# Last projection, norm and stores in two halves of 256 columns, with the second chunk's norm and the last gate on the vector engine

## The chip, the cores and the metric

The kernel runs on one core of a Trainium2 chip. The core has five engines that work side by side, each through its own list of instructions in the order in which the program gives them: TensorE (PE, matrix products), VectorE (DVE), ScalarE (ACT), GpSimd (POOL) and SyncE (SP, which here only issues transfers). Semaphores tie the lists together. Transfers between the core's memory and the chip's main memory go through 16 DMA engines; ACT can issue some too. The metric is the device time of one execution in microseconds (us).

## The reference

A trunk of two layers over 2048 positions of 1024 numbers each. The first layer is a gated short convolution. The second is a stick-breaking attention of 8 heads of 64, strictly causal, whose result is gated, projected back to 1024, added to the residual stream and normed:

```python
def _rmsnorm(x, g):
    xf = x.astype(jnp.float32)
    y = xf * lax.rsqrt(jnp.mean(xf * xf, axis=-1, keepdims=True) + RMS_EPS)
    return (y * g.astype(jnp.float32)).astype(x.dtype)
...
        z = jnp.einsum("bhqd,bhkd->bhqk", qb, kf[:, :, :kl]) * scale
        q_pos = q0 + jnp.arange(Q_BLOCK)
        mask = jnp.arange(kl)[None, :] < q_pos[:, None]
        log_one_minus = jnp.where(mask, jax.nn.log_sigmoid(-z), 0.0)
        rev = lax.cumsum(log_one_minus, axis=3, reverse=True)
        weights = jnp.exp(jnp.where(mask, z + rev, -jnp.inf))
        outs.append(jnp.einsum("bhqk,bhkd->bhqd", weights, vf[:, :, :kl]))
```

All numbers are float32. The change is in the very last steps: gate, output projection, residual addition, final norm, stores.

## The kernel before

**Layout.** Features lie on the 128 partitions, positions along the columns. The positions are cut into four chunks of 512, c = 0 to 3, which are worked in this order; the last chunk, c = 3, is the one with which the program ends. The residual stream of a chunk is 8 tiles of 128 x 512 (`x2_c_i` holds two of them; `x` in the profile). A float32 product is made of three products of parts: each operand is split into a high and a low part (`mm3`: high by high, high by low, low by high), so an output tile of the last projection is 4 x 3 = 12 matmuls of 512 columns, and a chunk has 8 x 12 = 96.

**Attention.** For each chunk and head, `attend` makes the scores (`z`), the scan (`R`), its transposes (`wt`, split into `wth` and `wtl`) and the products with the values (`av`). The result of a pair of heads is a tile `ot`; `gate_kept` adds a first-value term (`v_first`) and multiplies by the gate (`sga`), and for c of 2 and 3 splits it into `og` (high and low part), the operand of the projection. The program's order is not the order of the heads: head 7's second half of chunk 3 is the last to be done.

**Projection and norm.** `out_kept` (c = 0 to 2) makes the 8 product tiles (`pob`), adds each to its `x` on DVE, squares it on ACT (`sq`), sums the squares on POOL (`acc`) and scales by the gain on ACT. `norm_kept` sums `acc` over the partitions with PE (`pst`: products with a column of ones), takes the reciprocal root by 12 small DVE steps (`v`, `t`, `yr`), spreads it over the partitions by four transposes (`prb`), multiplies the 8 tiles and stores them by SP. The multiplication is POOL's for c of 0 and 1, from a copy of `prb` (`pbs`) that ACT makes, and DVE's for c = 2, straight from `prb`.

`out_last` does both for c = 3: squares of the first five tiles are summed by POOL into `acc`, those of the other three go to PE straight away, so that PE does four tiles of sums at the end. Its multiplications are six by DVE and two (k = 2 and 6) by POOL, which reads a second broadcast copied by ACT. Its stores go in turn to SP and ACT.

**What sets the order.** Every operation is first recorded with the name of its part: `a37` is head 7 of chunk 3, `g33` the gate of its fourth tile, `o2` and `n2` projection and norm of chunk 2, `o3` the last projection with its norm. `places` gives each operation a number, between the two numbers of its part in the table PLAN; `order` then runs through all operations with estimated durations, always takes the one that can start first (by that number where several can), and so fixes one list for each engine. `emit` (line 363) writes them out, so line 363 stands in every row of the profile. Behind all of them the program reads a flag (`some`) and branches on it (line 1409); the branch isn't taken in this run.

Of the kernel before, what the change touches and what calls it, by code (L numbers as in the profile page):

```python
# [10 lines left out]
F32 = mybir.dt.float32  # L11
# [5 lines left out]
P = 128  # L17
# [354 lines left out]
def kernel(  # L372
# [891 lines left out]
    def gate_kept(c, k, ot):  # L1264
        sg = load_sg(c, k)
        by_block = ot.rearrange("p (j k) -> p j k", j=4)
        nc.gpsimd.tensor_add(by_block, by_block, v_first[:, c, k, :].unsqueeze(2).to_broadcast([P, 4, P]))
        nc.gpsimd.tensor_mul(ot, ot, sg)
        if c < 2:
            nc.sync.dma_start(out=og_d[c][k], in_=ot)  # L1270
        else:
            split_og(c, k, ot)
# [31 lines left out]
    def norm_kept(c):  # L1304
        pb = rstd_bcast(acc_b[c], f"x2{c}")
        if c < 2:
            pbs = t512(f"pbs_{c}")
            nc.scalar.copy(pbs, pb)
        for k, x in enumerate(x2_t[c]):
            if c < 2:  # L1310
                nc.gpsimd.tensor_mul(x, x, pbs)
            else:
                nc.vector.tensor_mul(x, x, pb)
            nc.sync.dma_start(out=outT[k * P:(k + 1) * P, cols(c)], in_=x)

    def out_last(c):

        x2 = x2_rows(c)
        acc = sb.tile([P, CH], F32, name=f"acc_x2{c}", tag="acc", bufs=2)
        ps2 = psum.tile([P, CH], F32, name=f"pst_x2{c}", tag="wt", bufs=NWT)  # L1320

        def add_sums(t, first, last):
            for j in range(4):
                nc.tensor.matmul(ps2[:, j:j + 1], t[:, j * P:(j + 1) * P], ones[:, 0:1], start=first and j == 0,
                                 stop=last and j == 3, skip_group_check=True)

        late = []
        for ob in range(KD):
            x = x2[ob]
            nc.sync.dma_start(out=x, in_=x1_d[c][ob])  # L1330
            tag, bufs = (("lin", NLIN), ("z", NZ))[ob % 2]
            ps = psum.tile([P, CH], F32, name=f"pob_{c}_{ob}", tag=tag, bufs=bufs)
            mm3(ps, wob[ob:ob + 1], og_t[c], kt=4)
# [5 lines left out]
            if ob < NACC:  # L1339
                square_into(acc, x, ob == 0, f"x2{c}{ob}", nc.gpsimd, ("wth", NWTS))  # L1340
            else:
                sq = sb.tile([P, CH], F32, name=f"sq_x2{c}{ob}", tag=("wth", "wtl")[ob % 2], bufs=NWTS)
                nc.scalar.activation(sq, x, AF.Square)
                late.insert(0, sq)
# [3 lines left out]
        y = rsqrt(ps2, f"x2{c}")  # L1348
        pb = bcast(y, f"x2{c}")
        pbs = t512(f"pbs_{c}")  # L1350
        nc.scalar.copy(pbs, bcast(y, f"x2{c}s"))
        for k in range(KD):
            if k in (2, 6):
                nc.gpsimd.tensor_mul(x2[k], x2[k], pbs)
            else:
                nc.vector.tensor_mul(x2[k], x2[k], pb)
            (nc.scalar if k % 2 else nc.sync).dma_start(out=outT[k * P:(k + 1) * P, cols(c)], in_=x2[k])
# [45 lines left out]
    part("o3", out_last, 3)  # L1403
# [43 lines left out]
```

## Time and profile before

| what | before |
|---|---|
| median of 3 runs | 1345.77 us (1344.04, 1347.22, 1345.77) |
| the profiled execution's own time | 1344.17 us |
| its span (first to last record) | 1342.4 us |
| PE busy | 1304.5 us, 97% |
| weight loads (PEld, beside PE) | 1079.2 us, 80% |
| DVE busy | 1015.8 us, 76% |
| ACT busy | 599.3 us, 45% |
| POOL busy | 435.6 us, 32% |
| DMA | 364.99 MB, mean 272 GB/s |

The share of busy time is over the whole span; the change touches its last 100 us. In the rows below and in the prediction, a group reads `out<-in` with the program's names, then partitions x elements; `x8` is a count; a releaser behind `<-` is what ended the idle time ahead of an instruction. A window's row gives its length, then busy time and count of PE, PEld, DVE, ACT and POOL, the granted PE clock as a share of full speed, the busy share of the DMA engines and the GB/s moved.

### The profile page before, as it was taken

To read this page: it belongs to the slowest core of one execution; us is meant where nothing else is said; L and a number is where in the kernel's file an instruction comes from. 1 tells how busy PE (TensorE), PEld (TensorE's weight loads), DVE (VectorE), ACT (ScalarE), POOL (GpSimd) and SP (SyncE) were. 2 spreads that over 40 slices of the span, in tenths; PEclk is the share of its full clock that TensorE was granted. 3 is DMA by queue.
4 is the path that set the end of the run, shared out by engine and by line. 5 is a ranking of instruction groups with operands and counts; after the bars stand their busy time and mean duration, and the time that the engine had idled before them with its cause. 6 is when DMAs were issued, how large, how long until landed. Compare 5 with 4: busy or idle time off the path is not lost.

```text
span 1342.4 us, 18964 instructions
## 1 busy us (share of the span) xinstructions
PE 1304.5 (97%) x6182; PEld 1079.2 (80%) x6182; DVE 1015.8 (76%) x1605; ACT 599.3 (45%) x1052; POOL 435.6 (32%) x553
## 2 busy tenths in 40 slices
PE   7999999999999999999999999999999999999996
PEld 5788888888888888888787778788778887788885
DVE  6899866689964654656869569877998886797855
ACT  7344434444431332223344334554555553566643
POOL 5252000001000000010032355234456675547982
PEclk9999999999999999999999999999999999999997
DMA  9539879878898799987999976887687567998734
GB/s 288 207 106 326 285 278 318 295 263 312 287 358 291 253 348 340 336 272 246 351 328 310 307 260 214 259 275 237 220 297 261 186 203 225 339 363 304 266 103 161
DMA packets 216348, 364.99 MB, mean 272 GB/s; under 512 B 18096, under 2 KB 102064, under 8 KB 216240
## 3 DMA queue, kind: packets, MB, share of 16 engines
q1 hardware_dynamic: 214464, 362.61, 79.5%
q10 hardware_dynamic: 1616, 1.05, 0.3%
q8 instruction: 51, 0.84, 0.2%
q14 instruction: 57, 0.47, 0.1%
q0 software_dynamic: 160, 0.02, 0.1%
HBM read 217.35 MB, written 146.28 MB: 271 GB/s over the span
## 4 chain that ended last, share of the span: by engine, by line
PE 79%; DVE 11%; issue 3%; DMA 3%; POOL 1%; ACT 1%; SPq 0%; DVEq 0%; POOLq 0%; ACTq 0%
PE fa_C L363 11%; PE fa_B L363 10%; PE pob L363 6%; PE fa_o L363 6%; PE fd_C L363 6%; PE fa_kq L363 5%; PE fd_B L363 5%; PE fa_vg L363 4%; PE fe_C L363 3%; PE fd_o L363 3%; PE fd_vg L363 3%; PE fe_B L363 3%; PE fd_kq L363 3%; PE av L363 2%; PE wt L363 2%
## 5 line engine op out<-in xcount | busy, mean ns | idle before, releaser
L363 POOL COPY halo<-p 128x2 f32<-128x2 f32 x32 | 15.1, 472 | 435.9 <-DVE p L363 435.8
L363 POOL TENSOR_TENSOR acc_x<-acc_x,sq_x 128x512 f32<-128x512 f32 x53 | 76.0, 1438 | 129.6 <-ACT sq_x L363 124.9
L363 PE MATMUL pob<-og,wob 128*128 128x512 f32 x384 | 103.9, 404 | 0.6 <-DVE x L363 0.6
L363 PE MATMUL fa_C<-op_t,whl_s_C 128*128 128x512 f32 x336 | 83.3, 390 | 0.0
L363 PE MATMUL fa_B<-op_t,whl_s_B 128*128 128x512 f32 x336 | 82.4, 390 | 0.2 <-ACT f_B L363 0.2
L363 PEld LDWEIGHTS pob<-og,wob 128*128 128x128 f32 x384 | 67.6, 189 | 11.9 <-DVE x L363 1.1
L363 DVE TENSOR_TENSOR_SCAN R<-R,ones 128x192 f32<-128x192 f32 x128 | 74.2, 621 | 3.2 <-POOL R L363 3.2
L363 PEld LDWEIGHTS fa_B<-op_t,whl_s_B 128*128 128x128 f32 x336 | 62.9, 188 | 13.6 <-ACT f_B L363 0.6
L363 PEld LDWEIGHTS fa_C<-op_t,whl_s_C 128*128 128x128 f32 x336 | 63.0, 188 | 13.1
L363 DVE SCALAR_TENSOR_TENSOR cv<-p,cw,cv 128x512 f32<-128x512 f32 x64 | 50.4, 788 | 11.0 <-ACT cv L363 8.4
L363 ACT CAST wth<-wt 128x512 fp32r<-128x512 f32 x64 | 36.5, 573 | 39.1 <-PE av L363 21.6
L363 ACT ACTIVATE sq_x<-x 128x512 f32<-128x512 f32 x56 | 35.1, 631 | 42.1 <-DVE x L363 30.9
L363 ACT ACTIVATE cv<-p,cw 128x512 f32<-128x512 f32 x32 | 23.2, 725 | 68.1 <-DVE p L363 68.1
L363 DVE TENSOR_TENSOR wtl<-wt,wth 128x512 fp32r<-128x512 f32 x64 | 42.5, 668 | 13.1 <-ACT wth L363 12.2
L363 PE MATMUL wt<-ident,R 128*128 128x128 f32 x248 | 46.6, 275 | 1.4 <-DVE R L363 1.4
L363 PE MATMUL fa_C<-op_b,whl_a_C 128*128 128x512 f32 x168 | 43.1, 390 | 0.0
L363 PE MATMUL fa_B<-op_t,whl_a_B 128*128 128x512 f32 x168 | 43.0, 390 | 0.0
L363 PE MATMUL fe_B<-op_b,whl_a_B 128*128 128x512 f32 x168 | 42.9, 390 | 0.0
L363 POOL TENSOR_SCALAR_AFFINE_SELECT R<-R 128x256 f32<-128x256 f32 x64 | 34.5, 547 | 24.7 <-ACT R L363 24.4
L363 PE MATMUL fd_C<-op_t,whl_s_C 128*128 128x512 f32 x168 | 42.3, 390 | 0.1
L363 PE MATMUL fe_C<-op_b,whl_a_C 128*128 128x512 f32 x168 | 42.0, 390 | 0.0
L363 PE MATMUL fd_C<-op_b,whl_s_C 128*128 128x512 f32 x168 | 41.8, 390 | 0.0
(1016 smaller groups left out, 3813.4 us busy)
## 6 DMA issues: line engine op xcount, KB each, us to landing
sw_s_C<-whl_s_C SPq DMA_DIRECT2D x32, 512.0 KB, 4.2
sw_s_B<-whl_s_B SPq DMA_DIRECT2D x32, 512.0 KB, 4.4
q<-q_d SPq DMA_DIRECT2D x32, 512.0 KB, 5.9
sw_a_C<-whl_a_C SPq DMA_DIRECT2D x24, 512.0 KB, 3.5
sw_a_B<-whl_a_B SPq DMA_DIRECT2D x24, 512.0 KB, 3.7
whl_s_C<-sw_s_C SPq DMA_DIRECT2D x24, 512.0 KB, 5.4
whl_s_B<-sw_s_B SPq DMA_DIRECT2D x24, 512.0 KB, 5.3
whl_s_o<-sw_s_o SPq DMA_DIRECT2D x24, 512.0 KB, 5.3
```

The source lines that it names most:

```text
L363: getattr(o.engine.engine, o.name)(*map(real, o.args), **{k: real(v) for k, v in o.kw.items()})
```

## The change

The last projection (`out_last`) is done twice, for columns 0 to 255 and for 256 to 511 of the last chunk, each time with its own sums, root, broadcast, multiplications and stores. A product tile is now 128 x 256, so there are 192 matmuls of 256 columns in place of 96 of 512, with a weight load each as before. A half has two columns of sums instead of four (`add_sums`), a root of two columns, a broadcast of two transposes. All eight multiplications of a half are DVE's; the second broadcast with its copy (`pbs`) and POOL's two multiplications are gone. The first half stores by SP alone, the second in turn by SP and ACT; a store is 128 KB, with rows of 1 KB.

The second chunk's norm (c = 1) is multiplied by DVE instead of POOL. The last gate (c = 3, k = 3) is done by DVE in four steps of 128 columns that add and multiply at once, instead of POOL's addition and multiplication. In PLAN, `o3` becomes `o30` and `o31`, and the numbers of `a06`, `a30`, `a31`, `a36`, `o0` and `o1` change.

```diff
@@ -54,19 +54,19 @@
...
-    "n2": (1218.33, 1322.06), "o3": (2272.7, 2273.2),
+    "n2": (1218.33, 1322.06), "o30": (2272.7, 2272.95), "o31": (2272.95, 2278.2),
...
@@ -1263,9 +1263,15 @@
 
     def gate_kept(c, k, ot):
         sg = load_sg(c, k)
-        by_block = ot.rearrange("p (j k) -> p j k", j=4)
-        nc.gpsimd.tensor_add(by_block, by_block, v_first[:, c, k, :].unsqueeze(2).to_broadcast([P, 4, P]))
-        nc.gpsimd.tensor_mul(ot, ot, sg)
+        if c == NCH - 1 and k == 3:
+            for b in range(4):
+                blk = slice(b * P, (b + 1) * P)
+                nc.vector.scalar_tensor_tensor(out=ot[:, blk], in0=ot[:, blk], scalar=v_first[:, c, k, b:b + 1],
+                                               in1=sg[:, blk], op0=ALU.add, op1=ALU.mult)
+        else:
+            by_block = ot.rearrange("p (j k) -> p j k", j=4)
+            nc.gpsimd.tensor_add(by_block, by_block, v_first[:, c, k, :].unsqueeze(2).to_broadcast([P, 4, P]))
+            nc.gpsimd.tensor_mul(ot, ot, sg)
         if c < 2:
             nc.sync.dma_start(out=og_d[c][k], in_=ot)
         else:
@@ -1303,58 +1309,64 @@
 
     def norm_kept(c):
         pb = rstd_bcast(acc_b[c], f"x2{c}")
-        if c < 2:
+        if c < 1:
             pbs = t512(f"pbs_{c}")
             nc.scalar.copy(pbs, pb)
         for k, x in enumerate(x2_t[c]):
-            if c < 2:
+            if c < 1:
                 nc.gpsimd.tensor_mul(x, x, pbs)
             else:
                 nc.vector.tensor_mul(x, x, pb)
             nc.sync.dma_start(out=outT[k * P:(k + 1) * P, cols(c)], in_=x)
 
-    def out_last(c):
-
-        x2 = x2_rows(c)
-        acc = sb.tile([P, CH], F32, name=f"acc_x2{c}", tag="acc", bufs=2)
-        ps2 = psum.tile([P, CH], F32, name=f"pst_x2{c}", tag="wt", bufs=NWT)
+    HC = CH // 2
+    x2_last = []
+
+    def out_last(c, hf):
+
+        if hf == 0:
+            x2_last.extend(x2_rows(c))
+            for ob in range(KD):
+                nc.sync.dma_start(out=x2_last[ob], in_=x1_d[c][ob])
+        at = slice(hf * HC, (hf + 1) * HC)
+        nm = f"x2{c}{hf}"
+        acc = sb.tile([P, CH], F32, name=f"acc_{nm}", tag="acc", bufs=2)[:, 0:HC]
+        ps2 = psum.tile([P, CH], F32, name=f"pst_{nm}", tag="wt", bufs=NWT)
 
         def add_sums(t, first, last):
-            for j in range(4):
+            for j in range(2):
                 nc.tensor.matmul(ps2[:, j:j + 1], t[:, j * P:(j + 1) * P], ones[:, 0:1], start=first and j == 0,
-                                 stop=last and j == 3, skip_group_check=True)
+                                 stop=last and j == 1, skip_group_check=True)
 
         late = []
         for ob in range(KD):
-            x = x2[ob]
-            nc.sync.dma_start(out=x, in_=x1_d[c][ob])
+            x = x2_last[ob][:, at]
             tag, bufs = (("lin", NLIN), ("z", NZ))[ob % 2]
-            ps = psum.tile([P, CH], F32, name=f"pob_{c}_{ob}", tag=tag, bufs=bufs)
-            mm3(ps, wob[ob:ob + 1], og_t[c], kt=4)
+            ps = psum.tile([P, CH], F32, name=f"pob_{c}_{ob}_{hf}", tag=tag, bufs=bufs)[:, 0:HC]
+            mm3(ps, wob[ob:ob + 1], [og[:, :, at] for og in og_t[c]], kt=4)
             if late:
                 add_sums(late.pop(), ob == NACC + 1, False)
             if ob == NACC:
                 late.append(acc)
             nc.vector.tensor_add(x, x, ps)
-            if ob < NACC:
-                square_into(acc, x, ob == 0, f"x2{c}{ob}", nc.gpsimd, ("wth", NWTS))
+            if ob == 0:
+                nc.scalar.activation(acc, x, AF.Square)
             else:
-                sq = sb.tile([P, CH], F32, name=f"sq_x2{c}{ob}", tag=("wth", "wtl")[ob % 2], bufs=NWTS)
+                sq = sb.tile([P, CH], F32, name=f"sq_{nm}{ob}", tag=("wth", "wtl")[ob % 2], bufs=NWTS)[:, 0:HC]
                 nc.scalar.activation(sq, x, AF.Square)
-                late.insert(0, sq)
+                if ob < NACC:
+                    nc.gpsimd.tensor_add(acc, acc, sq)
+                else:
+                    late.insert(0, sq)
             nc.scalar.activation(x, x, AF.Copy, scale=gains["f"][:, ob:ob + 1])
         while late:
             add_sums(late.pop(), False, not late)
-        y = rsqrt(ps2, f"x2{c}")
-        pb = bcast(y, f"x2{c}")
-        pbs = t512(f"pbs_{c}")
-        nc.scalar.copy(pbs, bcast(y, f"x2{c}s"))
+        pb = bcast(rsqrt(ps2, nm, n=2), nm, n=2)[:, 0:HC]
+        o = S - CH * (c + 1) + hf * HC
         for k in range(KD):
-            if k in (2, 6):
-                nc.gpsimd.tensor_mul(x2[k], x2[k], pbs)
-            else:
-                nc.vector.tensor_mul(x2[k], x2[k], pb)
-            (nc.scalar if k % 2 else nc.sync).dma_start(out=outT[k * P:(k + 1) * P, cols(c)], in_=x2[k])
+            x = x2_last[k][:, at]
+            nc.vector.tensor_mul(x, x, pb)
+            (nc.scalar if hf and k % 2 else nc.sync).dma_start(out=outT[k * P:(k + 1) * P, o:o + HC], in_=x)
 
 
     def part(name, f, *args):
@@ -1400,7 +1412,8 @@
     for c in range(3):
         part(f"o{c}", out_kept, c)
         part(f"n{c}", norm_kept, c)
-    part("o3", out_last, 3)
+    for hf in range(2):
+        part(f"o3{hf}", out_last, 3, hf)
     nc.on = False
     ops = nc.order(PLAN)
     with tc.manual_schedule():
```

Three places show what this does to the lists of instructions. In the names, the number behind a tile is a counter; `pob_7` before is the eighth product tile, `pob_7_1` after the eighth of the second half.

PE, end of the program. Before, the last product tile is followed by four tiles of sums with four columns each, and by two broadcasts:

```order
L363 MATMUL pob_7_13128<-og_3_13025,wob_11711 128x512 x3
L363 MATMUL pst_x_13150<-ones,acc_x_13058 128x1 x4
L363 MATMUL pst_x_13150<-ones,sq_x_13139 128x1 x4
L363 MATMUL pst_x_13150<-ones,sq_x_13152 128x1 x4
L363 MATMUL pst_x_13150<-ones,sq_x_13163 128x1 x4
L363 MATMUL prb_x_13189<-ident,yr_x_13178 128x128 x4
L363 MATMUL prb_x23s<-ident,yr_x_13178 128x128 x4
```

After, the end of the second half:

```order
L363 MATMUL pst_x_13312<-ones,acc_x_13197 128x1 x2
L363 MATMUL pob_7_1_13317<-og_0_12837,wob_11711 128x256 x3
L363 MATMUL pob_7_1_13317<-og_1_12568,wob_11711 128x256 x3
L363 MATMUL pob_7_1_13317<-og_2_12712,wob_11711 128x256 x3
L363 MATMUL pob_7_1_13317<-og_3_13021,wob_11711 128x256 x3
L363 MATMUL pst_x_13312<-ones,sq_x_13322 128x1 x2
L363 MATMUL pst_x_13312<-ones,sq_x_13328 128x1 x2
L363 MATMUL pst_x_13312<-ones,sq_x_13344 128x1 x2
L363 MATMUL prb_x_13364<-ident,yr_x_13353 128x128 x2
```

The first of four tiles of sums now stands ahead of the last product tile, each tile has two columns, and there is one broadcast of two transposes. All sums and the broadcast of the first half stand further up, among the second half's products.

DVE, from the split of the last attention's weights to the last gate (`ot_3`). Before:

```order
L363 TENSOR_TENSOR wtl_6_1_12901<-wt_6_1_12882,wth_6_1_12893 128x512
L363 TENSOR_TENSOR x_2_3_12629<-x_2_3_12629,pob_7_12880 128x512
L363 TENSOR_TENSOR wtl_7_1_12934<-wt_7_1_12889,wth_7_1_12927 128x512
L363 TENSOR_TENSOR ot_3_12931<-ot_3_12931,av_6_12783 64x512
L363 TENSOR_TENSOR ot_3_12931<-ot_3_12931,av_7_12949 64x512
L363 TENSOR_SCALAR v_x_13023<-pst_x_13016 128x4
```

After:

```order
L363 TENSOR_TENSOR wtl_6_1_12861<-wt_6_1_12841,wth_6_1_12850 128x512
L363 TENSOR_TENSOR x_1_0_12012<-x_1_0_12012,prb_x_12857 128x512 x2
L363 TENSOR_TENSOR x_1_1_12073<-x_1_1_12073,prb_x_12857 128x512 x2
L363 TENSOR_TENSOR x_1_2_12160<-x_1_2_12160,prb_x_12857 128x512 x2
L363 TENSOR_TENSOR x_1_3_12194<-x_1_3_12194,prb_x_12857 128x512 x2
L363 TENSOR_TENSOR x_2_2_12563<-x_2_2_12563,pob_5_12830 128x512
L363 TENSOR_TENSOR x_2_3_12591<-x_2_3_12591,pob_6_12872 128x512
L363 TENSOR_TENSOR wtl_7_1_12933<-wt_7_1_12883,wth_7_1_12911 128x512
L363 TENSOR_TENSOR ot_3_12919<-ot_3_12919,av_6_12805 64x512
L363 TENSOR_TENSOR x_2_3_12591<-x_2_3_12591,pob_7_12930 128x512
L363 TENSOR_TENSOR ot_3_12919<-ot_3_12919,av_7_12950 64x512
L363 SCALAR_TENSOR_TENSOR ot_3_12919<-ot_3_12919,v_first,sga_3_11075 128x128 x4
```

The eight multiplications of the second chunk's norm (`x_1_0` to `x_1_3`) now stand ahead of the split `wtl_7_1` of the last head, and the gate stands behind the two additions to `ot_3` as four steps.

PE, around the first use of `og_3`, the last gate's result. Before, from the third chunk's sums on:

```order
L363 MATMUL pst_x_13016<-ones,acc_x_12704 128x1 x4
L363 MATMUL pob_5_13006<-og_1_12608,wob_11669 128x512
L363 MATMUL pob_5_13006<-og_2_12710,wob_11669 128x512 x3
L363 MATMUL pob_0_12924<-og_3_13025,wob_11312 128x512
L363 MATMUL pob_1_12947<-og_3_13025,wob_11330 128x512
L363 MATMUL pob_2_12979<-og_3_13025,wob_11367 128x512
L363 MATMUL pob_3_12994<-og_3_13025,wob_11628 128x512
L363 MATMUL pob_0_12924<-og_3_13025,wob_11312 128x512 x2
L363 MATMUL pob_1_12947<-og_3_13025,wob_11330 128x512 x2
```

After:

```order
L363 MATMUL pst_x_13011<-ones,acc_x_12673 128x1 x4
L363 MATMUL pob_5_0_13018<-og_0_12837,wob_11669 128x256 x3
L363 MATMUL pob_5_0_13018<-og_1_12568,wob_11669 128x256 x3
L363 MATMUL pob_5_0_13018<-og_2_12712,wob_11669 128x256 x2
L363 MATMUL pob_0_0_12970<-og_3_13021,wob_11312 128x256
L363 MATMUL pob_1_0_12907<-og_3_13021,wob_11330 128x256
L363 MATMUL pob_2_0_12987<-og_3_13021,wob_11367 128x256
L363 MATMUL pob_3_0_12925<-og_3_13021,wob_11628 128x256
L363 MATMUL pob_5_0_13018<-og_2_12712,wob_11669 128x256
L363 MATMUL pob_5_0_13018<-og_3_13021,wob_11669 128x256
L363 MATMUL pob_0_0_12970<-og_3_13021,wob_11312 128x256 x2
L363 MATMUL pob_1_0_12907<-og_3_13021,wob_11330 128x256 x2
```

In both, the products with `og_3` are put off behind those of other tiles that need only `og_0` to `og_2`; after, those tiles are half as wide, so the same count of products lasts half as long.

10 rows, old and new, of the table PLAN are left out of this document.

## The prediction

> **What bounds the kernel now.** I read the stretches of the span first, then the chain of work that ended last, then the queues of the last 40 us. The stretches (length, then busy time and count of PE, PEld, DVE, ACT and POOL, granted clock, DMA share, GB/s) say where TensorE (PE) stops being full:
>
> ```profile
> 1315.00:1324.00 9.00, 9.00 (x46) 7.54 (x44) 7.57 (x13) 6.49 (x12) 5.17 (x4) 1.00 0.65 234
> 1324.00:1343.00 19.00, 5.08 (x34) 4.62 (x33) 5.75 (x19) 2.39 (x4) 2.49 (x2) 0.56 0.33 116
> ```
>
> Up to 1324 PE is busy all the time; behind it lie 19 us in which it does 5. So there are two regions: a dense stream, which gets shorter only by less matrix work, and a tail of dependent steps. The chain (start, length, what) shows their border:
>
> ```profile
> core 0 of [0], span 1342.4 us
> ...
> 1301.31 1.11 PE av L363 x10
> 1302.42 7.11 PE pob L363 x31
> 1309.53 0.79 PE pst_x L363 x8
> 1310.31 4.42 PE pob L363 x19
> 1314.73 0.44 PE prb_x L363 x4
> 1315.17 8.22 PE pob L363 x36
> 1323.39 3.76 PE pst_x L363 x32
> 1327.15 0.02 issue
> 1327.18 0.17 DVE v_x L363
> ...
> 1329.66 1.10 PE prb_x L363 x4
> ...
> 1330.85 0.70 DVE x L363
> ```
>
> From 1301.31 to 1323.39 each PE piece begins where the one before it ends: no wait is left in the stream. Call 1323.39, the end of the last projection matmul, **E**. Behind E: sums of squares on PE (3.76 us), the reciprocal root on DVE (1327.18 to 1329.66), its broadcast by PE (to 1330.85), the multiplications, the last store. The last multiplication is POOL's, and the last store of the SP queue waits for it:
>
> ```profile
> 1334.82 0.33 SPq L363 DMA_DIRECT2D out_dram<-x  x1
> ```
> The span ends at 1342.4, 7.58 us after that issue. Three rows say what lies in between: the landing of the last SP store (KB, us from issue), the queue's wait behind it, and the DMA engines (share, GB/s) in those microseconds:
>
> ```profile
> out_dram<-x SPq DMA_DIRECT2D x1, 256.0 KB, 5.2
> ```
> ```profile
> SPq L1409 <- SPq L1409: 3.8, 1, 3.8
> ```
> ```profile
> 1334.00:1338.00 4.00, 0.00 (x0) 0.00 (x0) 0.53 (x1) 0.00 (x0) 0.79 (x1) 0.50 1.02 370
> ```
>
> Line 1409 is the program's closing read of a flag and its branch, which SP does once its last store is issued; behind the branch SP stands 3.8 us for nothing but itself. With some 1.5 us for the read that is 1340.2. The stores, at 370 GB/s with the engines full until 1338, land at 1334.82 + 5.2 = 1340.0. Both are there 2.4 us before the end, and this profile can't say which one counts. I take the branch, since a wait on itself is no wait on bytes, and carry the 7.58 us over.
>
> **The change part by part.** All terms are for the profiled execution: 1344.17 us, of which 1342.4 are the span and 1.8 lie around it. The median of the runs shown is 1345.77, 1.6 us above; I apply the difference to the median.
>
> *1. The stream before E gets longer.* First, 96 matmuls of 512 columns become 192 of 256. The 512 form takes 8.22 us for 36 = 0.228 us, in the 31 before it 0.229. The trace has no 256-wide matmul of this projection, but it has the attention's, each with a weight load of its own; here are the first of six in a row, and the matmul behind the sixth:
>
> ```profile
> 1301.15 0.28 PE L363 MATMUL av<-wth,vv 128*128 128x256 f32 x1
> ...
> 1301.86 0.22 PE L363 MATMUL av<-wth,vv 128*128 128x128 f32 x1
> ```
>
> 0.71 us for six starts is 0.118 us each. From below the nearest row is a 192-wide one, four in 0.44 us, 0.110 each:
>
> ```profile
> 1232.17 0.44 PE z L363 x4
> ```
>
> The upper end is the whole 512 form, 0.229. I take 0.118, the same width: 192 x 0.118 - 96 x 0.229 = 22.7 - 22.0 = **+0.7 us**. At 0.110 it would be -0.9; above 0.118 every 0.005 costs 1 us.
>
> Here one rule of the Trainium skill speaks against the change. These are the weight loads under those matmuls (PEld):
>
> ```profile
> 1301.27 0.19 PEld L363 LDWEIGHTS av<-wth,vv 128*128 128x128 f32 x1
> ```
>
> This load (1301.27 to 1301.46) lies under the matmul that started at 1301.26, one of the six, and the starts do not spread. The Trainium skill, "TensorE: Matmul & The Clock Gate", Part 3, The mechanism, says that a weight load overlaps running matmuls only when it is for another group of rows of the array. By that rule the 0.19 us would stand in the open 192 times instead of 96 times, some 18 us more, and the change would lose; the trace contradicts it at 256 columns.
>
> Second, work that stood behind E moves ahead of it: the first half's sums (4 tiles x 2 matmuls) and the second half's first tile (2 matmuls). Four such matmuls (8 records) take 0.79 us, so ten take **+2.0 us**. Third, the first half's broadcast, two transposes at 0.11: **+0.2 us**. Together E comes **2.9 us later**, if no wait is added.
>
> *2. The tail behind E gets shorter.* Step by step, before and after:
> - E to the root's first step: before 1327.18 - 1323.39 = 3.79 us: ACT was behind, since DVE had done the third chunk's norm just before, and 32 records of sums lay there. After: add, square, and one tile's sums. Half-wide DVE and ACT operations are not in the trace. These groups (busy us, mean ns of one) bound them:
>
> ```profile
> L363 DVE TENSOR_TENSOR x<-x,prb_x 128x512 f32<-128x512 f32 x14 | 8.5, 684 | 1.3 <-PE prb_x L363 1.3
> ...
> L363 DVE TENSOR_TENSOR wtl<-wt,wth 128x384 fp32r<-128x384 f32 x8 | 4.4, 553 | 1.8 <-ACT wth L363 1.7
> ```
> ```profile
> L363 ACT ACTIVATE sq_x<-x 128x512 f32<-128x512 f32 x56 | 35.1, 631 | 42.1 <-DVE x L363 30.9 <-DMA whl_a_o<-sw_a_o 6.1 <-issue 1.6
> ...
> L363 ACT CAST wth<-wt 128x384 fp32r<-128x384 f32 x8 | 3.8, 480 | 10.3 <-PE av L363 8.7 <-PE wt L363 1.6
> ```
>
> DVE loses 0.131 us with 128 columns, so 256 take 0.42 (between half of 0.684 and 0.553); ACT's square likewise 0.42 (between 0.32 and 0.48). Then 0.04 + 0.42 + 0.03 + 0.42 + 0.1 + four records, about 0.6 = 1.6 us: **-2.2 us**. The two tiles of sums ahead of it run under the add and the square (0.79 us under 0.9).
> - The root: the same 12 small steps, 2.48 us to the broadcast: 0.
> - Broadcast: four transposes, 1329.66 to 1330.85, become two; at 0.21 us less each: **-0.4 us**. They run at half clock now, and I leave them there:
>
> ```profile
> 1327.00:1328.00 1.00, 0.14 (x1) 0.05 (x1) 0.69 (x5) 0.00 (x0) 0.00 (x0) 0.50 0.00 0
> ```
>
> - Multiplications to the last issue: before 1334.82 - 1330.85 = 3.97 us, DVE with six and, beside it, POOL with two. After: eight of 256 columns, all on DVE. The norm of the third chunk gives the pace of such a row:
>
> ```profile
> 1315.34 4.87 DVE L363 TENSOR_TENSOR x<-x,prb_x 128x512 f32<-128x512 f32 x8
> ```
>
> (4.87 - 0.68) / 7 = 0.60 us per 512 columns, 0.26 less for 256 by the slope above: 0.34. 7 x 0.34 + 0.42 + 0.03 = 2.8 us (2.5 at half of 0.60, 3.8 at the 384-wide 0.47): **-1.2 us**.
>
> The tail goes from 19.0 to 15.2 us, **-3.8**. Sum: +2.9 - 3.8 = **-0.9**; SP issues the seventh store and ACT the eighth, which may give 0.3 back, so **-1.0 us**. Bounds: matmul price -1.5 to +1.2 (0.110 to 0.124), half-wide DVE and ACT together -0.4 to +1.1.
>
> *3. Second chunk's norm and last gate on DVE.* POOL (start, length) had them:
>
> ```profile
> 1294.74 10.11 POOL L363 TENSOR_TENSOR x<-x,pbs 128x512 f32<-128x512 f32 x8 [1.05 <-ACT pbs L363]
> ...
> 1308.27 1.32 POOL L363 TENSOR_TENSOR ot<-ot,sga 128x512 f32<-128x512 f32 x1
> ```
> ```profile
> 1290.00:1315.00 25.00, 25.00 (x135) 21.16 (x133) 10.32 (x30) 9.57 (x17) 17.04 (x14) 1.00 0.49 168
> ```
>
> The gate ended at 1309.59, 7.2 us after the last head (1302.42), and PE did not wait: 35 products and 4 sums lay in between (35 x 0.229 + 0.79 = 8.8 us). After the change 33 half-wide ones and the sums do, 4.7 us. The gate needs ACT's copy 0.63, DVE's add 0.68, four pieces of 128 columns (between the 0.17 of a 4-wide step and 0.42; 0.3 each) and ACT's cast 0.63 = 3.1 us. Cover left: 1.6 us. The second norm costs DVE 4.9 us, where it was busy for 10.3 of 25; queued behind it are two adds and the split for the last head, and the chain above shows the head's ten products (1301.31) behind other matrix work, so PE has some in reserve. I cost part 3 at nothing. The loads of the last chunk now follow all the norm's stores on SP; the norm ends earlier, so they are not later. The stores have rows half as long; the tail needs 8 x 128 KB at the pace of the multiplications, and the 7.58 us cover them.
>
> **Rivals.**
> - *PE waits for DVE in the stream.* Third norm, first half's adds and root share DVE's queue. After the norm's 4.9 us come two adds, two squares on ACT, then the first half's last sums; my count puts them on time with 0.3 us to spare. The last gate also reads two operands in SBUF beside POOL's adds. How that can go:
>
> ```profile
> 1283.70 1.27 DVE L363 TENSOR_SCALAR yr_x<-t_x 128x4 int32<-128x4 int32 x1
> ```
> ```profile
> 1283.12 3.19 POOL L363 TENSOR_TENSOR acc_x<-acc_x,sq_x 128x512 f32<-128x512 f32 x2
> ```
>
> A 4-wide step took 1.27 instead of 0.17 us beside POOL's adds. One such loss is covered (1.1 of 1.6), two are not. The Trainium skill, "GPSIMD Engine Reference", Key points, says that POOL shares its SBUF interfaces with DVE instructions that have two SBUF inputs; the trace agrees, and shows it for small one-input steps too. Price 0.5 to 2 us of waits: net -0.5 to +1.0, about 1346.
> - *The other side: half-wide matmuls do not hold 0.118.* In the trace at most six stand in a row; here it is 192, with a weight load each. From 0.123 on the gain is gone (192 x 0.005 = 1.0). At 0.14 the stream costs 4.2 us more: +3.2, 1349. Against it: nothing in those six starts drifts.
> - *The end hangs on the bytes.* Behind the first multiplication 2.1 MB go out now (5.7 us at 370 GB/s); after, 1.05 MB, 2.8 us, the time of the multiplications. The last store would land about 2.5 us after its issue instead of 5.2. If the landing sets the end, or if the code behind the branch comes late because the DMA engines are full, up to 2.7 us more go; I take half, 1.4: -2.4, 1343.4. For it: engines full until 1338. Against it: SP's 3.8 us on itself.
> - *It does not do what it says*: the last half's sums could wait for other work and the tail stay near 19 us: +2.9, 1348.7. DVE's order has the first half's multiplications before the last three adds, and they end 1 us ahead of E by the prices above, so this is unlikely.
>
> **How the numbers follow.** Forecast (-1.0, 1344.8) 0.52; bytes 0.22; waits in the stream 0.16; dearer matmuls 0.06; long tail 0.04. Own range of the forecast: -2.5 to +0.5. With the bytes, the waits, the bounds and the spread of three runs (1344.04 to 1347.22) I give 1342.2 to 1347.4. 0.2% is 2.7 us, about what a measurement of this kernel can tell from no change: faster than that in a little under half of the bytes' case and a fifth of the forecast's, 0.20; slower in the dearer matmuls and half of the long tail, 0.08; the same 0.72.
>
> **What would show it.** In the profile after: the 256-wide products 0.118 us apart; E 2.9 us later and without a wait of PE on DVE before it; E to the root's first step 1.6 us; first multiplication to last issue 2.8 us; end 7.3 to 7.6 us after SP's last issue (5 if the bytes set it). Products over 0.123 apart, or a wait of PE for `x` or `og` over 1 us, would make it wrong.

## The result and the profile after

| | before | after |
|---|---|---|
| median, 14 runs each | 1344.08 us | 1345.98 us |
| profiled execution | 1344.17 us | 1346.06 us |
| its span | 1342.4 us | 1344.3 us |

The ratio of after to before is **1.0018, 95% interval 1.0010 to 1.0026**: about 2.4 us slower, where the prediction had the likeliest case 1.0 us faster. The time lies inside the range, the sign is wrong. That it lies inside owes something to luck: the forecast started from a median of 1345.77 us in three runs, and the 14 runs of before have 1344.08.

First the tail, since it was the aim. These are PE's pieces at the end of the changed kernel (start, length; in brackets the idle time ahead of a piece and what ended it):

```profile
1320.37 4.55 PE L363 MATMUL pob<-og,wob 128*128 128x256 f32 x36
1324.77 0.38 PE L363 MATMUL prb_x<-ident,yr_x 128*128 128x128 f32 x2
...
1327.73 0.50 PE L363 MATMUL pst_x<-ones,acc_x 128*128 128x1 f32 x4
1328.09 1.67 PE L363 MATMUL pob<-og,wob 128*128 128x256 f32 x12
1329.60 0.95 PE L363 MATMUL pst_x<-ones,sq_x 128*128 128x1 f32 x8
1330.78 0.61 PE L363 MATMUL pst_x<-ones,sq_x 128*128 128x1 f32 x4 [0.23 <-ACT sq_x L363]
1333.89 0.41 PE L363 MATMUL prb_x<-ident,yr_x 128*128 128x128 f32 x2 [2.51 <-DVE yr_x L363]
```

E, the end of the last product, is now 1329.60, taken where the sums behind it start. DVE, SP and ACT behind it:

```profile
1331.42 0.16 DVE L363 TENSOR_SCALAR v_x<-pst_x 128x2 f32<-128x2 f32 x1 [1.21 <-PE pst_x L363]
...
1334.41 2.74 DVE L363 TENSOR_TENSOR x<-x,prb_x 128x256 f32<-128x256 f32 x8 [0.66 <-PE prb_x L363]
```
```profile
1336.93 0.56 SPq L363 DMA_DIRECT2D out_dram<-x  x1
```
```profile
1337.58 0.46 ACTq L363 DMA_DIRECT2D out_dram<-x  x1
```

The eight multiplications take 2.74 us, ACT issues the last store at 1337.58, and from E to the end of the span it is 14.7 us. In the same view of before (the timeline of PE) E is at 1323.23 (the prediction took 1323.39 from the chain):

```profile
1323.23 0.95 PE L363 MATMUL pst_x<-ones,acc_x 128*128 128x1 f32 x8
```

So the tail was 19.2 us there: **the tail got 4.5 us shorter**, more than forecast. The loss must lie ahead of E. The view of PE's waits from 1240 us on (us in all, times, longest) shows it, first of after, then of before:

```profile
PE prb_x L363 <- DVE yr_x L363: 2.5, 1, 2.5
PE pob L363 <- DVE og L363: 1.7, 1, 1.7
PE av L363 <- DVE wtl L363: 1.2, 2, 1.0
PE pst_x L363 <- ACT sq_x L363: 0.2, 1, 0.2
PE pob L363 <- ACT og L363: 0.2, 1, 0.2
```
```profile
PE prb_x L363 <- DVE yr_x L363: 2.5, 1, 2.5
PE pob L363 <- DVE x L363: 0.6, 1, 0.6
PE av L363 <- DVE wtl L363: 0.2, 1, 0.2
```

The 2.5 us belongs to the tail in both. The 0.6 us for an `x` stands just ahead of 1240 us; after has it too, 0.65 us at 1238, outside this view. New are 1.7 us for `og` and 1.0 us for `wtl`. They do not lie near the last gate, for which the prediction had looked, but 74 and 57 us ahead of the end, where the third chunk's projection starts and in its middle:

```profile
1267.83 0.73 PE L363 MATMUL pob<-og,wob 128*128 128x512 f32 x2 [0.15 <-ACT og L363]
1270.28 2.07 PE L363 MATMUL pob<-og,wob 128*128 128x512 f32 x4 [1.72 <-DVE og L363]
1272.15 1.67 PE L363 MATMUL z<-kt,q 128*128 128x192 f32 x8
...
1286.79 0.45 PE L363 MATMUL av<-wtl,vv 128*128 128x256 f32 x2 [0.98 <-DVE wtl L363]
```

And behind the first wait the products are slow: four of 512 columns and eight of 192 take 3.4 us, where the same ones take 1.9 us in e7 below. The stretches of after (length, busy times, granted PE clock behind the counts) tell why:

```profile
1269.00:1270.00 1.00, 0.00 (x0) 0.00 (x0) 1.00 (x1) 0.66 (x2) 0.93 (x2) 1.00 1.04 399
1270.00:1273.00 3.00, 2.72 (x9) 2.34 (x9) 2.44 (x3) 0.00 (x0) 3.00 (x5) 0.51 0.73 278
```

The granted clock is 0.51 for the three microseconds from 1270, the end of the wait. So this wait costs twice: while it lasts, and afterwards.

**The sum.** Both kernels do the same work in the same order up to a product that waits a little for `wtl`:

```profile
1242.71 0.39 PE L363 MATMUL av<-wtl,vv 128*128 128x256 f32 x1 [0.22 <-DVE wtl L363]
```
```profile
1244.33 0.39 PE L363 MATMUL av<-wtl,vv 128*128 128x256 f32 x1 [0.21 <-DVE wtl L363]
```

The first row is of after, which is 1.62 us ahead there, the second of before. From this point to E before takes 1323.23 - 1244.33 = 78.90 us and after 1329.60 - 1242.71 = 86.89, +7.99 us:

| term | us | from |
|---|---|---|
| narrow products | +1.5 | 36 in 1324.77 - 1320.37 = 4.40, 0.1222 each; 192 x 0.1222 - 96 x 0.229 |
| sums and transposes ahead of E | +2.0 | five tiles of sums 0.36 + 0.37 + 0.81 (two) + 0.36 = 1.9, transposes 1324.90 - 1324.77 = 0.13 |
| waits | +2.85 | 1.72 + 0.98 + 0.15 |
| half clock | +1.45 | 3.40 us here, 1.95 us for the same pieces in e7 below |
| together | +7.8 | of 7.99 |

The whole: -1.62 + 7.99 - 4.47 = +1.90, the difference of the two spans. What after has in hand at the common point is not the change's, since the order of work is the same up to there. Before runs at half clock near 733 and near 791 us, after in neither place (the first of these rows is before's, the second after's):

```profile
733.00:736.00 3.00, 3.00 (x9) 2.32 (x8) 3.00 (x17) 1.00 (x2) 0.00 (x0) 0.51 0.84 277
```
```profile
733.00:736.00 3.00, 3.00 (x14) 2.45 (x14) 3.00 (x15) 1.14 (x2) 0.00 (x0) 1.00 0.91 278
```

The runs below have one of these stretches, both or none, with the same order of work up to there (e12 and e14 apart, whose order differs from 965 us on). So beside each ratio stands the time from the common point to the end of the span, which is free of that: before 98.1 us, after 101.6. It is the time of one execution each and scatters too: e13 has before's order of work until a read near the end, and takes 100.4 us, 1.3 us of them in two waits that before does not have. Differences of some 2 us in this column say nothing by themselves.

### The profile page after: what moved, and what is told of

The parts are those of the page before. It is cut to its first block, busy times and chain, and to the rows that moved or that the text cites. A ratio compares the mean times of both kernels' runs of the same rounds, so it can differ in the third digit from the quotient of the medians.

```text
span 1344.3 us, 19213 instructions
## 1 busy us (share of the span) xinstructions
PE 1302.4 (97%) x6274; PEld 1081.0 (80%) x6274; DVE 1030.6 (77%) x1647; ACT 601.0 (45%) x1066; POOL 421.5 (31%) x545
## 5 line engine op out<-in xcount | busy, mean ns | idle before, releaser
L363 POOL TENSOR_TENSOR acc_x<-acc_x,sq_x 128x512 f32<-128x512 f32 (+1 forms) x57 | 75.3, 1324 | 145.0 <-ACT sq_x L363 142.8
L363 PE MATMUL pob<-og,wob 128*128 128x512 f32 (+1 forms) x480 | 107.7, 362 | 2.5 <-DVE og L363 1.7
L363 PEld LDWEIGHTS pob<-og,wob 128*128 128x128 f32 x480 | 74.2, 191 | 11.6 <-DVE og L363 2.2
L363 ACT ACTIVATE sq_x<-x 128x512 f32<-128x512 f32 (+1 forms) x63 | 36.2, 583 | 41.4 <-DVE x L363 33.2
```

What stands on the lines that cost most here:

```text
L363: getattr(o.engine.engine, o.name)(*map(real, o.args), **{k: real(v) for k, v in o.kw.items()})
```

## The experiments

| run | what | ratio to before, 95% | common point to end, us |
|---|---|---|---|
| before | | 1 | 1342.4 - 1244.33 = 98.1 |
| after | | 1.0018 (1.0010 to 1.0026) | 1344.3 - 1242.71 = 101.6 |
| e1 | after, old PLAN numbers | 1.0092 (1.0077 to 1.0108) | 1350.9 - 1243.79 = 107.1 |
| e2 | before, new PLAN numbers | 1.0043 (1.0030 to 1.0057) | 1345.2 - 1241.33 = 103.9 |
| e3 | halves alone | 1.0051 (1.0037 to 1.0065) | 1348.1 - 1243.80 = 104.3 |
| e4 | DVE norm and gate alone | 1.0009 (1.0000 to 1.0018) | 1343.2 - 1243.33 = 99.9 |
| e5 | before, new number of o1 | 1.0028 (1.0017 to 1.0040) | 1345.9 - 1243.69 = 102.2 |
| e6 | after, og_0 summed last | 0.9997 (0.9988 to 1.0006) | 1342.3 - 1244.51 = 97.8 |
| e7 | after, wait filled with work | 1.0013 (1.0004 to 1.0022) | 1346.0 - 1245.13 = 100.9 |
| e9 | before, narrow products alone | 1.0004 (0.9995 to 1.0013) | 1343.4 - 1243.83 = 99.6 |
| e11 | e6, flag read earlier | 0.9995 (0.9986 to 1.0004) | 1341.9 - 1243.88 = 98.0 |
| e12 | e11, three tiles wide | 0.9991 (0.9982 to 1.0000) | 1341.1 - 1242.77 = 98.3 |
| e13 | before, flag read earlier | 1.0001 (0.9991 to 1.0011) | 1341.8 - 1241.42 = 100.4 |
| e14 | e12, flag read as before | 0.9987 (0.9976 to 0.9998) | 1340.1 - 1241.73 = 98.4 |

### e1 and e2: the PLAN numbers apart from the code

e1 is the changed kernel with these six numbers of before, e2 the kernel before with the six new ones:

```diff
-"a06": (978.812, 995.727), "a30": (1616.85, 1772.16), "a31": (1514.38, 1685.5)
-"a36": (1593.54, 2009.97), "o0": (1349.96, 1416.95), "o1": (1486.8, 1705.74)
+"a06": (978.812, 996.346), "a30": (1602.58, 1772.16), "a31": (1514.38, 1692.57)
+"a36": (1593.52, 2009.95), "o0": (1346.61, 1413.6), "o1": (1527.61, 1746.55)
```

> The changed kernel with the six changed PLAN numbers of a06, a30, a31, a36, o0 and o1 set back to those of before; halves, DVE norm and DVE gate stay. Theory A (the new numbers cost: PE waits 1.72 us for the split og and 0.98 us for a split wtl in chunk 2 and 3, and the clock is halved for 3.4 us behind the first, about 1.5 us more): these waits are gone, 4.3 us faster than the changed kernel, ratio to before about 0.9994. Rival B (the halves themselves cost it: 256-wide matmuls and second set of sums): as slow as the changed kernel, ratio 1.0018, and the profile has waits of PE behind 1290 us.

> The kernel before with the six new PLAN numbers alone; one piece of 512 columns, norm and gate by POOL as before. Theory A: the waits of PE for og (1.7 us) and wtl (1.0 us) and the half clock behind them appear, ratio to before about 1.003 (+4 us). Rival B: no change, 1.000.

e2 shows the new waits to the hundredth, in a kernel that has none of the rest of the change:

```profile
1268.87 1.24 PE L363 MATMUL pob<-og,wob 128*128 128x512 f32 x4 [1.72 <-DVE og L363]
1285.53 0.45 PE L363 MATMUL av<-wtl,vv 128*128 128x256 f32 x2 [0.98 <-DVE wtl L363]
```

So the numbers alone bring them: theory A for the waits. The stretch is 5.8 us longer than before's: the three waits of after (2.85), some 1.45 of half clock, and two waits of about 0.5 us each in the third chunk's root and the last sums, which after does not have. But e1 refutes A's other half. Without the new numbers the changed kernel isn't 4 us faster but 9 us slower still (1354.86 us). Rival B named the place, behind 1290 us, but not the size. PE waits there, later and longer:

```profile
1308.80 0.65 PE L363 MATMUL prb_x<-ident,yr_x 128*128 128x128 f32 x4 [2.96 <-DVE yr_x L363]
...
1315.34 0.86 PE L363 MATMUL pob<-og,wob 128*128 128x256 f32 x5 [2.61 <-DVE x L363]
```
```profile
1310.08 4.87 DVE L363 TENSOR_TENSOR x<-x,prb_x 128x512 f32<-128x512 f32 x8
1314.87 1.74 DVE L363 TENSOR_TENSOR x<-x,pob 128x256 f32<-128x256 f32 x5
```

With the old numbers the third chunk's broadcast stands in PE's list at a place where its root isn't ready, and then DVE does the eight multiplications of that norm in one go (4.87 us, the second fence) while the half-wide products, which fill their tiles in half the time, wait for their additions. The granted clock is 0.5 behind each of the two waits. **The halves need other PLAN numbers, and the new numbers move the wait from the end to the third chunk's start, at a lower price.**

### e3 and e4: the two parts of the code apart

e3 has only the halves (the gate and the second norm by POOL), e4 only the two on DVE; both with the old numbers.

> The two halves alone, with the old PLAN numbers; norm of the second chunk and last gate by POOL as before. Theory A: stream +3.6 us by the changed kernel's profile (256-wide matmuls 0.123 apart, ten more sums, two transposes), tail -4.3 us: ratio 0.9994; a POOL gate has less cover from half-wide products, which may add a wait of up to 1 us (1.0002). Rival B: 1.0018 or more.

> Norm of the second chunk and last gate by DVE alone, old PLAN numbers, no halves. Theory A: both are covered by PE's work, ratio 1.000 (within 0.0004). Rival C (DVE becomes late for the last head's split behind 4.9 us of norm): PE waits 1 us or more for wtl or og_3, ratio 1.0008 or more.

e3 fails by its POOL. The sums of the third chunk wait for it, then the last gate, and the clock is 0.50 until 1315 (first PE's pieces, then POOL's):

```profile
1307.78 1.05 PE L363 MATMUL pst_x<-ones,acc_x 128*128 128x1 f32 x8 [2.77 <-POOL acc_x L363]
1309.65 5.06 PE L363 MATMUL pob<-og,wob 128*128 128x256 f32 x22 [0.82 <-ACT og L363]
```
```profile
1294.19 10.09 POOL L363 TENSOR_TENSOR x<-x,pbs 128x512 f32<-128x512 f32 x8 [1.05 <-ACT pbs L363]
1304.24 1.27 POOL L363 TENSOR_TENSOR acc_x<-acc_x,sq_x 128x512 f32<-128x512 f32 x1
```

Ten microseconds of the second norm on POOL push its last additions to `acc` behind 1304. With half-wide products PE is at these sums 61.2 us behind the common point (1307.78 - 2.77 - 1243.80), before at 65.0 (1309.37 - 1244.33): wide products covered the additions, half-wide ones do not. That the halves need the moves to DVE is a reading of these rows and not shown by the times: with the old numbers the halves with the moves (e1, 1.0092) are slower than without (e3, 1.0051), and no run has the halves with the new numbers and POOL. e4 has 1.8 us more in the profile, within the scatter; 1.06 us of it are one wait for an `x` behind the third norm, the rest isn't traced. Its ratio, 1.0009 (1.0000 to 1.0018), holds theory A's 1.000 as well as rival C's 1.0008, and the wait is at another place than C named (neither `wtl` nor `og_3`).

### e5: one number

```diff
-"o1": (1527.61, 1746.55)
+"o1": (1486.8, 1705.74)
```

> The kernel before with one new PLAN number, that of o1 (projection of the second chunk, 41 units earlier). Theory A1: this number alone uses up the second chunk's products that covered the third chunk's first gate, so PE's wait of 1.7 us for the split og and the half clock behind it (about 1.5 us) appear; ratio to before 1.0024. Rival: it takes both o1 and a30, no wait, 1.000.

The ratio, 1.0028, is what A1 had, its mechanism isn't: no wait of 1.7 us and no half clock at 1270. A row of smaller waits stands there and further on, 0.57 and 0.52 us for `x` and `og` near 1271, 0.37 for `wtl`, 0.65 for the flag's sum and 0.53 for the third root. The number makes this stretch tight; the one long wait, in e2, takes the other numbers too.

### e6: the wait taken away

In the changed kernel the first two tiles of the third chunk's projection are summed in another order, the late operand last:

```diff
-            mm3(ps, wob[ob:ob + 1], og_t[c], kt=4)
+            mm3(ps, wob[ob:ob + 1], og_t[c], kt=4, ks=(1, 2, 3, 0) if c == 2 and ob < 2 else None)
```

> The changed kernel, with the first two product tiles of the third chunk summed in the order og_1, og_2, og_3, og_0, so that nine products stand between the end of the second chunk and the first use of the late og_0. Theory A: the wait of 1.72 us and the half clock behind it vanish, 3.2 us or more faster than the changed kernel, ratio to before 0.9994, or 0.999 if the 1 us wait for the split wtl goes as well. Rival B (the half-wide products and second sums are the loss): no gain, 1.0018.

PE's list at this place, after and in e6:

```text
L363 MATMUL z_6_1_12605<-kt_6_12267,q_3_6_12256 128x192 x4
-L363 MATMUL pob_0_12617<-og_0_12612,wob_11312 128x512
-L363 MATMUL pob_1_12619<-og_0_12612,wob_11330 128x512
-L363 MATMUL pob_0_12617<-og_0_12612,wob_11312 128x512 x2
+L363 MATMUL pob_0_12611<-og_1_11977,wob_11312 128x512 x3
+L363 MATMUL pob_0_12611<-og_2_12023,wob_11312 128x512 x3
+L363 MATMUL pob_0_12611<-og_3_12197,wob_11312 128x512 x3
+L363 MATMUL pob_0_12611<-og_0_12615,wob_11312 128x512 x3
```

The waits of e6 there:

```profile
1272.12 1.20 PE L363 MATMUL pob<-og,wob 128*128 128x512 f32 x4 [0.29 <-DVE og L363]
```

Of 1.72 us 0.29 is left, the wait of 0.98 for `wtl` is gone, the clock stays up, and the stretch to the end is 97.8 us instead of 101.6. The ratio is 0.9997 (0.9988 to 1.0006) against 1.0018 (1.0010 to 1.0026): **another order in the sums of two tiles takes the loss away**, and Rival B falls. The planner orders some of the work behind it anew, too (the first half's sums come in one go where after has three pieces), so this edit moves more than the one operand. But the waits gone (1.72 + 0.15 + 0.98 - 0.29 = 2.56 us) and the half clock (1.45) make 4.0 us, and the stretch got 3.8 shorter. It also shows what the halves bring when nearly nothing waits: 0.3 us in the profile, no difference that the times can tell.

### e7: the same wait, filled

Seven more 512-wide products in the wait, into a tile that the next product begins anew:

```diff
+            if c == 2 and ob == 0:
+                for _ in range(7):
+                    nc.tensor.matmul(ps, wob[0][:, 0, 1, :], og_t[c][1][:, 0, :], start=True, stop=True)
             mm3(ps, wob[ob:ob + 1], og_t[c], kt=4)
```

> The changed kernel with seven extra 512-wide matmuls ahead of the first product that waits for og_0, into the same tile, which that product then begins anew; they stand in the 1.72 us wait. Theory G (idle PE is what halves the granted clock): the wait is full of work, the clock stays at 1.00 from 1264 to 1275 us, and the 1.5 us that the half clock took come back: ratio to before 1.0007. Rival: the clock falls for another reason, at the same place: 1.0018 or a little more.

```profile
1269.93 2.24 PE L363 MATMUL pob<-og,wob 128*128 128x512 f32 x9
1272.74 1.21 PE L363 MATMUL pob<-og,wob 128*128 128x512 f32 x4 [0.57 <-DVE og L363]
1273.79 1.04 PE L363 MATMUL z<-kt,q 128*128 128x192 f32 x8
1274.66 0.27 PE L363 MATMUL wt<-ident,R 128*128 128x128 f32 x1
1274.69 1.65 PE L363 MATMUL pob<-og,wob 128*128 128x512 f32 x6
```
```profile
1264.00:1275.00 11.00, 10.43 (x61) 8.75 (x60) 10.04 (x12) 6.79 (x13) 10.97 (x17) 1.00 0.86 289
```

`og` comes no earlier, 3.32 us behind the last `z` piece's start (1269.42) as in after (1270.28 - 1267.01 = 3.27). But the clock is 1.00 throughout, and the four wide products, eight `z` and the transpose behind it take 1.95 us (1272.74 to 1274.69) instead of 3.40. That agrees with theory G, and 1.45 us is the half clock's part; it is one execution, and the last section has a pair of equal waits of which one lost the clock and one did not, so it doesn't show it alone. In the time, 1.0013 against 1.0018, it can't be told: some 0.7 us were lost again by the end of this run (101.6 - 100.9 = 0.7 gained of 1.45).

### e9: the narrow form alone

```diff
-            mm3(ps, wob[ob:ob + 1], og_t[c], kt=4)
+            for k in range(4):
+                for w, m in ((0, 0), (0, 1), (1, 0)):
+                    for at in (slice(0, CH // 2), slice(CH // 2, CH)):
+                        nc.tensor.matmul(ps[:, at], wob[ob][:, w, k, :], og_t[c][k][:, m, at],
...
```

> The kernel before, whose last projection does each of its 96 products as two of 256 columns into the same tile, and nothing else: the price of the narrow form alone. By the changed kernel's spacing (0.1225 us) 192 x 0.1225 - 96 x 0.2285 = +1.6 us, ratio 1.0012; by the prediction's 0.118 +0.7 us, 1.0005; by a rule under which each weight load stands in the open, +18 us, 1.013.

```profile
1313.60 10.08 PE L363 MATMUL pob<-og,wob 128*128 128x256 f32 x82
1323.51 0.95 PE L363 MATMUL pst_x<-ones,acc_x 128*128 128x1 f32 x8
```

82 in 1323.51 - 1313.60 = 9.91 us are 0.121 each; the common point to the end is 1.5 us longer than before, which is within the scatter. The time, 1.0004 (0.9995 to 1.0013), holds both 1.0005 and 1.0012 and excludes 1.013. 192 products with a load of 0.191 us (mean) each show that the loads do not stand in the open. The Trainium skill, "TensorE: Matmul & The Clock Gate", Part 3, The mechanism, states the rule that the prediction gave, but ahead of it names a background weight buffer, beside another row group, as what lets a load run ahead. The trace agrees so far that these loads run ahead; which buffer they go to no run here shows.

### e11 to e14: a better version, and the end

e11 is e6 with the flag read ahead of the last multiplications, e13 the same edit on the kernel before:

```diff
-        nc.emit(ops)
+        cut = next(i for i, o in enumerate(ops) if o.part == "o31" and o.name == "tensor_mul")
+        nc.emit(ops[:cut])
     some = tc.nc.values_load(flag.real()[0:1, 0:1])
+        nc.emit(ops[cut:])
```

> The kernel of e6 (changed kernel, og_0 summed last), with the closing read of the flag put ahead of the second half's multiplications instead of behind the last store. If the end is the chain last store, flag read (0.6 to 0.8 us on SP and ACT), branch (3.9 us), the read's time goes: 0.7 us faster than e6, ratio to before 0.9992. If the landing of the stores sets the end, nothing changes: 0.9997.

> The kernel before with the flag read ahead of the multiplications of the last norm. SP and ACT read for 1.1 us behind the last store; by the chain through the branch the end comes 1.1 us earlier, ratio 0.9992. If the bytes of the last stores set the end (their landing at 1340.0 of 1342.4), nothing changes or only 0.2 us, 0.9999.

Neither moves the time by what can be told, and neither decides: e11's interval (0.9986 to 1.0004) holds both of its expectations, and so does e13's (0.9991 to 1.0011). In e11 SP's wait on itself behind the branch grows from 3.3 us (e6) to 4.6; and PE's wait for the root grows from 2.51 to 2.95 us, as in e12 and e13. e13's profile has two more waits (0.35 us near 1261 and 0.97 near 1264) that before does not have. Which of the two, the branch or the landing of the stores, sets the end is left open: in before they end at 1340.2 and 1340.0 by the prediction's reading, and no run here parted them.

e12 lets the first three of the last chunk's eight tiles be 512 wide, for 36 wide and 120 narrow products, with other PLAN numbers fitted to that; e14 is e12 without the flag's edit:

```diff
+        for ob in range(KD if hf == 0 else 0):
+            if ob >= NWIDE:
+                break
...
+            ps = psum.tile([P, CH], F32, name=f"pob_{c}_{ob}", tag=tag, bufs=bufs)
+            mm3(ps, wob[ob:ob + 1], og_t[c], kt=4)
...
+        for ob in range(NWIDE, KD):
```

> As e11, and the first three product tiles of the last chunk stay 512 wide (36 wide, 120 narrow products instead of 192 narrow), with PLAN numbers fitted to it. The narrow form's price falls from 1.6 to 1.0 us; if the first half's norm still fits beside the second half's products, 0.6 us faster than e11, ratio 0.9987. If DVE gets late with the first half's multiplications, no gain or a loss, 0.9995.

> The kernel of e12 with the flag read back behind the last store; three wide tiles, five in halves, og_0 summed last. If the early read cost what it gained (e11 and e12 show PE's wait for the root at 2.95 instead of 2.51 us), the time stays, ratio to before 0.9991 (1342.4); if the read set the end it is 0.7 us slower than e12, 0.9996. The wait for the root is 2.51 us again in both.

e14 has the lowest ratio, 0.9987 (0.9976 to 0.9998), just clear of 1; with twelve variants measured that is weak evidence of a gain. It can't be told from e12's 0.9991 (0.9982 to 1.0000), and each of the two intervals holds both numbers that were expected of it. Its wait for the root is 2.51 us again. Why it would be faster isn't shown: its stretch from the same product is 98.4 us, no shorter than before's 98.1, it still waits 0.46 us for `og` and 0.86 us for `wtl`, and its fitted PLAN also differs ahead of that point.

## Why the prediction was wrong

- **The step that failed: "if no wait is added"**, in part 1, with part 3's "I cost part 3 at nothing". The cover was counted at the last gate and at the tail, and there it held: PE waits nowhere for `og_3`, and the first half's last sums are on time. At the gate that was close to luck. Its four pieces, put at 0.3 us each, took 2.27 us, with POOL's addition beside them:

```profile
1305.69 2.27 DVE L363 SCALAR_TENSOR_TENSOR ot<-ot,v_first,sga 128x128 f32<-128x128 f32 x4
```

  ACT's cast of the gate ended at 1308.61, and the first product with `og_3` came near 1309.0 (the eighth behind the sums' end at 1308.00): some 0.35 us of cover were left, not 1.6. But the new PLAN numbers move work from 1245 us on, and the order of 1245 to 1290 was not followed step by step. There the third chunk's first operand `og_0` is split by DVE from 1268.62 to 1270.22, at a place where PE has run out of other products. Before, the same split ended at 1268.40 and the third chunk's first product came at 1270.37:

```profile
1267.28 1.12 DVE L363 TENSOR_TENSOR og<-ot,og 128x512 fp32r<-128x512 f32 x1
...
1270.37 1.87 PE L363 MATMUL pob<-og,wob 128*128 128x512 f32 x7
```

  and after:

```profile
1268.62 1.60 DVE L363 TENSOR_TENSOR og<-ot,og 128x512 fp32r<-128x512 f32 x1
```
```profile
1268.41 1.26 POOL L363 TENSOR_TENSOR acc_x<-acc_x,sq_x 128x512 f32<-128x512 f32 x1
```

  The split takes 1.60 us, since POOL's addition runs beside it until 1269.67. Before it took 1.12, also beside one; the splits of `og` that have no POOL addition beside them take 0.66 to 0.69 us in both traces. That is the effect that the first rival named. That rival had the mechanism, "PE waits for DVE in the stream", but put it at the last gate and the first half's sums and priced it at 0.5 to 2 us; it cost 2.85 us of waits and 1.45 us of half clock. The half clock stood in no term.
- **Narrow products:** taken at 0.118, they are 0.122 apart (e9: 0.121): +1.5 us instead of +0.7, between the prices of 0.110 and 0.124. Not the 0.14 of the rival, and no rule that puts the loads in the open.
- **Sums and transposes ahead of E:** +2.2 forecast, 2.0 measured. Right.
- **The tail:** -3.8 forecast, -4.5 measured (19.2 to 14.7). E to the root 1.82 us (1.6 forecast), the root 2.47 (2.48 before), broadcast to the first multiplication 0.52 (before 1.19, so -0.7 instead of -0.4: the two transposes ran at a granted clock of 1.00 here, and at 0.50 in e6, where it is 0.76), first multiplication to SP's last issue 2.52 (2.8 forecast; ACT's last issue follows at 3.17), SP's last issue to the end 7.4 instead of 7.58. The half-wide square on ACT, put at 0.42, took 0.42, but by luck: the rows shown lose 0.151 us with 128 columns and would have given 0.33.
- **The end on the bytes:** the last store lands 2.7 us after its issue on SP and 4.0 us on ACT, instead of 5.2. The 7.4 us from SP's last issue to the end are what the forecast had (7.3 to 7.6), not the 5 of this rival; from the last issue of all, now ACT's, it is 6.7. Which of the two readings is right is open all the same (e11, e13).
- **Without the waits** (e6) the change does nearly what the sum of the other steps says: 97.8 us against 98.1, 0.3 us instead of 1.0 to the good. E comes 82.8 us behind the common point (1327.27 - 1244.51), +3.9 instead of +2.9, with the narrow products' 0.8 and a wait of 0.29 in it; the tail is 15.0 us, -4.1 instead of -3.8.

## What to carry to other kernels

Where a change comes with a new order, follow every stretch from the first row that differs, not only those that the code change names: here the order that made room at the end took the cover from somewhere else. Halving the width of products nearly halves the time that each covers (0.229 to 0.122 us), so everything that used to hide behind them (a norm on a slow engine, a gate, a split) has to be counted anew. When an operand comes late, sum its products last before moving anything else; that cost nothing here and took the ratio from 1.0018 to 0.9997, which is more than the change itself brings.

## What the runs showed of the hardware

A wait of 1.72 us was followed by half clock for the next three microseconds (after and e2), waits of 2.96, 2.61 and 2.77 us were too (e1, e3), waits of 0.98 and 1.06 us were not. It is not a matter of length alone. Near 790 us, where these kernels have the same order of work, PE waits 1.81 us in after and keeps its clock; in e4 it waits 1.80 us at the same product and loses it (first after, then e4; each time the wait, then the clock):

```profile
790.08 0.96 PE L363 MATMUL fa_o<-op_t_('o', 2)_0_6478,whl_s_o 128*128 128x512 f32 x3 [1.81 <-DVE x L363]
```
```profile
791.00:794.00 3.00, 3.00 (x15) 2.47 (x14) 3.00 (x6) 1.77 (x3) 0.00 (x0) 1.00 0.22 87
```
```profile
789.51 0.98 PE L363 MATMUL fa_o<-op_t_('o', 2)_0_6478,whl_s_o 128*128 128x512 f32 x3 [1.80 <-DVE x L363]
```
```profile
791.00:794.00 3.00, 3.00 (x9) 2.27 (x9) 2.93 (x6) 1.39 (x4) 0.00 (x0) 0.54 0.19 75
```

And the half clock of before near 733 follows no long wait: the longest one there is 0.64 us, ahead of eight products of one column, and after keeps its clock with the same 0.63 us at the same place.

```profile
730.53 1.05 PE L363 MATMUL pst_x<-ones,acc_x 128*128 128x1 f32 x8 [0.64 <-POOL acc_x L363]
```

The Trainium skill, "TensorE: Matmul & The Clock Gate", Part 1, says that the clock is set by how busy PE has been, in a window of some 3.4 us that runs freely; by that, it would depend on where in the window a gap falls. This fits equal gaps of which one passes and one doesn't. Its advice under Why this matters for your kernels, to avoid gaps of more than about 3 us, is not enough here: 1.72 us sufficed, and the measurement decides. In this kernel, which is full of PE work, the wait of 1.72 us cost 1.45 us more by the half clock behind it, and the stretches of half clock near 733 and 791 us, which some executions have and others not, are one source of the scatter between executions of one program.
